# Eight key pages of the last sample in the first four attention steps, two each, and the last pair's values later

## The chip, the cores and the metric

The kernel runs on one core of one Trainium2 chip. The core has a matmul engine (TensorE, PE in the profile, its weight loads PEld), a vector engine (VectorE, DVE), a scalar engine (ScalarE, ACT), GpSimd (POOL), SyncE (SP), which here only issues loads and stores, and 16 DMA engines. Each engine takes its instructions in the order of its own queue. The metric is the device time of one execution in microseconds; lower is better. The kernel before takes 1068.47 us, the median of three runs (1067.93 to 1070.03).

## What is computed

One layer of a decoder trunk, for a prompt of 512 positions and for 8 samples of one new position each, with shared weights. The reference, cut:

```python
h = rms_norm(x, norm1_g) * (1.0 + sc1) + sh1
z = h @ w_in
xr, gr, q, k, v, fl, ga, gb = jnp.split(z, cuts, axis=-1)
xc, conv_new = causal_dwconv(xr, conv_buf, conv_w, conv_b)
hr, h_last = rg_lru(xc, h0, pos0, rg_wr, rg_br, rg_wi, rg_bi, rg_lambda)
ya = (hr.astype(x.dtype) * jax.nn.gelu(gr)) @ w_proj_a
logf = jax.nn.log_sigmoid((fl + b_f).astype(jnp.float32))
yb = attend(q, k, v, logf).reshape(B, T, ATTN_W) @ w_proj_b
mixed = (jax.nn.sigmoid(ga) * ya + jax.nn.sigmoid(gb) * yb) @ w_o
x = x + g1 * mixed
gu, up = jnp.split(h2 @ w_ffn_in, 2, axis=-1)
x = x + g2 * ((jax.nn.silu(gu) * up) @ w_ffn_out)
```

`attend` is attention with a decay from the sums of `logf`: for the prompt over its own 512 keys, for a sample over its own key and 1024 past ones. The past keys and values lie in a paged cache, 8 pages of 128 rows for each sample; a page of keys or values is 128 x 1024 floats, 512 KB:

```python
k_all = jnp.concatenate([cache_k[page_table].reshape(DB, P, N_HEADS, HEAD_DIM).astype(k.dtype), k], axis=1)
s = jnp.einsum("bqhd,bkhd->bhqk", q, k_all, preferred_element_type=jnp.float32) * scale
s = s + Fk[:, :, P:, None] - Fk[:, :, None, :]
p = jax.nn.softmax(s, axis=-1)
return jnp.einsum("bhqk,bkhd->bqhd", p.astype(v_all.dtype), v_all)
```

## The kernel before

**Products.** All large products take the 512 prompt positions and the samples together, 520 columns in two halves of 260. Operands are split in a high and a low part of 32 bits, so a product of 8 blocks of 128 rows is 2 x 8 x 3 = 48 matmuls (L245). They run in one fixed order and are numbered by `begin`: 0 and 1 are the last of `q`, then `xr` (input of the recurrence), the gate products `ga` and `gb` of the merge, and `gr`, mixed, up to 31; 32 is the first `k`; 33 to 39 and 41 are the projection `pa` of the recurrence's branch, with the first `v` between. Then come eight attention steps, then the merge (`pb`), `w_o` and the FFN.

**Weights.** A chunk of weight columns is loaded by SP into `wraw` (two buffers). ACT makes its high part `whi` (L210), DVE subtracts to give `wlo` (L211), three buffers each. `begin` runs this ahead of the product that needs it, by an estimate of time in `reach`.

**Key pages.** For the samples' past keys, a page is loaded, multiplied on DVE with the sample's query, which was broadcast to 128 partitions (`qb`, L639 and L648), and reduced by heads into `S`: two instructions of DVE a page, L667 and L668 (L663 and L664 where an entry is two half pages: the 16 entries of samples 0 and 1, each with two loads of 256 KB; samples 2 to 7 have 48 whole pages). `tick`, called by `begin` for products 0 to 41 and three or four times in an attention step, does in this order: `key_sums` for the entries loaded long enough ago, the next stage of a softmax chain, then values, then the loads of new value and key pages. `KEYS[n]` says how many key entries product n loads. Before, all 64 are loaded by product 40. `issue_after(state["last"])` ties the sums behind the last `wlo` in DVE's order.

**Softmax and values.** Samples go in pairs r = 0 to 3. When a pair's 16 pages are summed, the chain `past_softmax` runs a stage at every second tick: decays added to `S` and a maximum (`mk`, L704 to L706), a transposing matmul `lgt` (L709), `st` and `dg` on DVE (L711, L713), a matmul `lgm` (L718), a subtraction (L719), exponentials, and the weights `pw`. Then the value pages are loaded and multiplied on PE (`pv`, L751), and DVE folds them into `dr` (L757, L759). `VALUES_AT` says at which of the four places of an attention step a value is taken.

**Page pool.** Key pages, value pages, `qb` of samples 2 to 7, and the blocks `araw` of the table product `ada` (L296, L308) share one pool of seven buffers of 128 x 1024. Each takes the buffer of the seventh before it. Loads of pages are issued by POOL up to product `LAST_POOL`, then by SP.

**Recurrence.** DVE makes the convolution `xc` (L894), ACT and DVE its high and low parts `xch` and `xcl` (L278, L279), PE the recurrence's gates (`gate`, L915); later DVE scans the recurrence and splits the result in `gh` and `gl`, the input of `pa`.

**An attention step i** splits the next head pair's query (`q_split`: `qqA`, `qqB` on ACT, `qlA`, `qlB` on DVE, L1079), broadcasts decay rows, and runs the next `k` product with the step's `v` tokens in its middle, then the next `v` product with scores in its middle, and the sum with the values. `k_product`'s evacuation puts the low half of k into `ksA` and `ksB` by DVE (L1059); DVE also splits the transposed probabilities (`pl`, L1164).

The order on each engine is set by a scheduler at build time, from the order of the code, the ties of `issue_after`, and its own estimates; so an edit of `KEYS` can also move instructions that it doesn't name.

Of the kernel before, what the change touches and what calls it, by code (L numbers as in the profile page):

```python
# [64 lines left out]
def kernel(ctx, tc, xT, par, gates, b_f, cst, cse, own, cache_k, cache_v, cache_lf, pt,  # L65
# [103 lines left out]
    def flush():  # L169
        while stores:  # L170
# [1 line left out]

    later = {}

    KEYS = dict(zip(range(42), (2, 2, 2, 0, 3, 3, 3, 2, 1, 1, 1, 1, 2, 2, 2, 1, 0, 1, 0, 1, 2, 2, 2, 2, 1, 1, 1, 1, 2, 2, 1, 2,
                                1, 2, 1, 2, 1, 2, 1, 2, 1, 0)))
    VALUES = (19, 21, 23, 25, 27, 29, 31, 35, 37, 39)
    LAST_POOL = 40

    def load_chunks(upto):  # L180
        while state["dma"] < len(chunks) and state["dma"] <= upto:
            c = state["dma"]
            raw = wp.tile([128, KT, 256], F32, name="wraw", tag="wraw", bufs=2)
            o = 0
            for src, r0, nk, c0, n in chunks[c]:
                sp.dma_start(raw[:, :nk, o:o + n],
                             src[r0:r0 + nk * 128, c0:c0 + n].rearrange("(k p) c -> p k c", p=128))
                o += n
            raws[c] = raw
            state["dma"] += 1  # L190

    def split_upto(n):
        while state["split"] < len(units) and state["split"] <= n:
            m = state["split"]
            c, o, nk = units[m]
            load_chunks(c)
            raw = raws[c]
            state["split"] += 1
            his, los = [], []
            step = 4 if m in in_heap else KT  # L200
            for k0 in range(0, nk, step):
                k1 = min(nk, k0 + step)
                if m in in_heap:
                    hi = slot("whs", 512, F32R).rearrange("p (k c) -> p k c", c=128)
                    lo = slot("wls", 512, F32R).rearrange("p (k c) -> p k c", c=128)
                else:
                    hi = wp.tile([128, KT, 128], F32R, name="whi", tag="whi", bufs=3)
                    lo = wp.tile([128, KT, 128], F32R, name="wlo", tag="wlo", bufs=3)
                src = raw[:, k0:k1, o:o + 128]
                state["act"] = act.copy(hi[:, :k1 - k0], src)  # L210
                state["last"] = dve.tensor_tensor(lo[:, :k1 - k0], src, hi[:, :k1 - k0].bitcast(F32), ALU.subtract)  # L211
# [441 lines left out]
    def key_sums():  # L653
        for p in pend:
            p[0] += 1
        while pend and pend[0][0] >= state["age"]:
            _, s, j, pg, q, half = pend.pop(0)
            r = s // 2
            c = 256 * (r % 2) + 32 * j + H * (s % 2)
            with tc.issue_after(state["last"].ins):  # L660
                if half is not None:
                    b, c = 8 * (r % 2) + j, H * (s % 2) + 8 * half
                    dve.tensor_tensor(pg, pg, q.unsqueeze(1).to_broadcast([128, 2, 512]), ALU.mult)  # L663
                    dve.tensor_reduce(S[r // 2].rearrange("p (b c) -> p b c", c=32)[:, b:b + 2, c:c + 8],  # L664
                                      pg.rearrange("p j (h d) -> p j h d", d=DH), AX.X, ALU.add)
                else:
                    dve.tensor_tensor(pg, pg, q, ALU.mult)  # L667
                    dve.tensor_reduce(S[r // 2][:, c:c + H], pg.rearrange("p (h d) -> p h d", d=DH), AX.X, ALU.add)  # L668
            summed[r] += 1
            if summed[r] == 2 * NPAGE:  # L670
                chains.append([9, past_softmax(r)])
# [401 lines left out]
    def q_split(i):  # L1073
        qq = slot("qqA", NP, F32R), slot("qqB", NP, F32R)
        ql = slot("qlA", NP, F32R), slot("qlB", NP, F32R)
        for a in range(2):
            t = kvs[i]["qr"][a]
            act.activation(qq[a], t, AF.Copy, scale=-(DH ** -0.5))
            dve.scalar_tensor_tensor(ql[a], t, -(DH ** -0.5), qq[a].bitcast(F32), ALU.mult, ALU.subtract)  # L1079
# [507 lines left out]
```

## Time and profile before

| what | value |
|---|---|
| median of three runs | 1068.47 us |
| lowest and highest | 1067.93 and 1070.03 us |
| profiled execution, its own time | 1067.71 us |
| profiled execution, its span | 1066.1 us |
| mean granted clock of TensorE | 0.987 |
| ACT busy | 494.2 us (46%) |
| POOL busy | 202.2 us (19%) |
| bytes moved | 206.95 MB, mean 194 GB/s |

The profile shows one execution. The 1.6 us between its span and its own time lie before the first and after the last instruction of the span. A row of the timeline gives start, duration, engine, line, operation, what is written and read, the shape, and in brackets how long the engine was idle before and what ended that. A row of the waits gives engine and line, what was waited for, the sum in us, how often, and the longest. In the page's slices each digit is the busy share, in tenths, of one of 40 equal parts of the span (26.65 us each).

### The profile page before, as it was taken

Reading aid. Unit: us, or ns where it says so; the run is one execution under the profiler, and the core shown is the slowest. Engines: PE = TensorE matmul, PEld = TensorE weight load, DVE = VectorE, ACT = ScalarE, POOL = GpSimd, SP = SyncE. Lnnn points to the kernel's source line nnn. Section 1 sums busy time; section 2 is a strip of 40 time slices with the busy share of each in tenths; the row PEclk is TensorE's granted clock in tenths of the full one; section 3 lists DMA queues with packets and bytes.
Section 4 is the critical chain, followed back from the end, with each engine's and each line's share of the span. In section 5 each row is a group of like instructions: output and inputs, shape, how many; then the busy total and the mean of one; then the engine's idle time right before and its main releaser. Section 6 shows DMA issues by size and latency. Waiting matters only on the chain.

```text
span 1066.1 us, 21006 instructions
## 1 busy us (share of the span) xinstructions
PE 1021.3 (96%) x8210; PEld 948.1 (89%) x8210; DVE 664.0 (62%) x1166; ACT 494.2 (46%) x976; POOL 202.2 (19%) x348
## 2 busy tenths in 40 slices
PE   4999899999999999999999999999999999999994
PEld 2888779999998987888898989999999999999993
DVE  5447999988999986656765447733343333443363
ACT  4423565757782367767783235523212232123251
POOL 0224511112134234544400014100000000000022
PEclk9999899999999999999999999999999999999998
DMA  9898887778788998987746852232333332332212
GB/s 327 281 320 286 279 297 208 260 240 297 255 283 280 351 314 263 259 252 250 248 172 216 313 166 70 73 88 79 109 90 80 97 102 80 95 104 80 72 55 74
DMA packets 165285, 206.95 MB, mean 194 GB/s; under 512 B 9778, under 2 KB 126018, under 8 KB 165122
## 3 DMA queue, kind: packets, MB, share of 16 engines
q1 hardware_dynamic: 147746, 149.90, 45.6%
q0 software_dynamic: 13760, 49.29, 13.6%
q10 hardware_dynamic: 3680, 6.42, 1.6%
q8 instruction: 64, 1.05, 0.4%
q14 instruction: 35, 0.29, 0.1%
HBM read 192.49 MB, written 13.09 MB: 193 GB/s over the span
## 4 chain that ended last, share of the span: by engine, by line
PE 76%; DVE 9%; issue 4%; DMA 4%; ACT 4%; POOL 2%; POOLq 1%; SPq 0%; ACTq 0%; DVEq 0%
PE fiu L245 11%; PE fig L245 11%; PE fo L245 9%; PE pb L245 4%; PE k L245 4%; PE v L245 4%; PE pa L245 3%; PE gr L245 3%; PE gb L245 3%; PE ga L245 3%; PE xr L245 3%; PE wo L245 3%; PE pv L751 3%; DMA wraw<-in_w_in_dram 2%; PE qp L467 2%
## 5 line engine op out<-in xcount | busy, mean ns | idle before, releaser
L211 DVE TENSOR_TENSOR wlo<-wraw,whi 128x1024 fp32r<-128x1024 f32 (+1 forms) x131 | 160.7, 1227 | 159.3 <-ACT whi L210 153.2
L210 ACT CAST whi<-wraw 128x1024 fp32r<-128x1024 f32 (+1 forms) x131 | 136.7, 1043 | 242.7 <-PE fo L245 74.6
L337 POOL TENSOR_TENSOR ss<-ss,sq 128x260 f32<-128x260 f32 x18 | 13.6, 756 | 419.5 <-ACT sq L336 419.0
L245 PE MATMUL fiu<-h2h,wlo 128*128 128x260 f32 x320 | 90.5, 283 | 0.0
L245 PE MATMUL fig<-h2h,wlo 128*128 128x260 f32 x320 | 90.5, 283 | 0.0
L245 PE MATMUL fig<-h2l,whi 128*128 128x260 f32 x320 | 90.2, 282 | 0.0
L245 PE MATMUL fiu<-h2l,whi 128*128 128x260 f32 x320 | 90.2, 282 | 0.0
L245 PE MATMUL fig<-h2h,whi 128*128 128x260 f32 x320 | 90.2, 282 | 0.0
L245 PE MATMUL fiu<-h2h,whi 128*128 128x260 f32 x320 | 90.2, 282 | 0.0
L245 PE MATMUL fo<-ach,whi 128*128 128x260 f32 x292 | 82.8, 284 | 0.0
L245 PE MATMUL fo<-ach,wlo 128*128 128x260 f32 x292 | 82.5, 282 | 0.0
L245 PE MATMUL fo<-acl,whi 128*128 128x260 f32 x292 | 82.3, 282 | 0.0
L622 POOL DMA_DIRECT2D pg<-in_cache_k_dram x79 | 42.1, 533 | 115.8 <-DVE S L668 61.1
L245 PEld LDWEIGHTS fiu<-h2h,whi 128*128 128x128 f32 x320 | 60.2, 188 | 0.0
L245 PEld LDWEIGHTS fig<-h2h,whi 128*128 128x128 f32 x320 | 60.2, 188 | 0.0
L245 PEld LDWEIGHTS fig<-h2l,whi 128*128 128x128 f32 x320 | 60.2, 188 | 0.0
L245 PEld LDWEIGHTS fiu<-h2l,whi 128*128 128x128 f32 x320 | 60.2, 188 | 0.0
L245 PEld LDWEIGHTS fig<-h2h,wlo 128*128 128x128 f32 x320 | 60.1, 188 | 0.0
L245 PEld LDWEIGHTS fiu<-h2h,wlo 128*128 128x128 f32 x320 | 60.1, 188 | 0.0
L667 DVE TENSOR_TENSOR pg<-pg,qb 128x1024 f32<-128x1024 f32 x48 | 57.4, 1213 | 1.1 <-DMA pg<-in_cache_k_dram 1.0
L668 DVE TENSOR_REDUCE S<-pg 128x16 f32<-128x1024 f32 x48 | 57.2, 1207 | 0.0
L245 PEld LDWEIGHTS fo<-ach,wlo 128*128 128x128 f32 x292 | 55.1, 189 | 0.0
(388 smaller groups left out, 3445.6 us busy)
## 6 DMA issues: line engine op xcount, KB each, us to landing
araw<-in_ada_w_dram SPq DMA_DIRECT2D x48, 512.0 KB, 6.3
pg<-in_cache_k_dram POOLq DMA_DIRECT2D x47, 512.0 KB, 5.6
wraw<-in_w_fi_dram SPq DMA_DIRECT2D x44, 512.0 KB, 4.0
pg<-in_cache_v_dram SPq DMA_DIRECT2D x42, 512.0 KB, 4.9
wraw<-in_w_in_dram SPq DMA_DIRECT2D x34, 512.0 KB, 8.4
wraw<-in_w_in_dram SPq DMA_DIRECT2D x11, 1024.0 KB, 7.9
pg<-in_cache_v_dram POOLq DMA_DIRECT2D x22, 512.0 KB, 5.5
pg<-in_cache_k_dram POOLq DMA_DIRECT2D x32, 256.0 KB, 5.4
```

The costliest lines, as they stand in the source:

```text
L210: state["act"] = act.copy(hi[:, :k1 - k0], src)
L211: state["last"] = dve.tensor_tensor(lo[:, :k1 - k0], src, hi[:, :k1 - k0].bitcast(F32), ALU.subtract)
L245: state["mm"] = pe.matmul(out[:, :HALF], lhsT=wt[k], rhs=at, start=k == 0 and m == 0, stop=k == nk - 1 and m == 2)
L337: eng.tensor_tensor(acc[:, t0:t1], acc[:, t0:t1], q_, ALU.add)
L467: state["mm"] = pe.matmul(b[:, :HALF], lhsT=wt, rhs=at[:, t0:t1], start=k == 0 and m == 0, stop=k == 3 and m == 2)
L622: done.append(eng.dma_start(pg, cache[bass.ds(r, 1), :, c0:c1].rearrange("a p c -> (a p) c")))
L667: dve.tensor_tensor(pg, pg, q, ALU.mult)
L668: dve.tensor_reduce(S[r // 2][:, c:c + H], pg.rearrange("p (h d) -> p h d", d=DH), AX.X, ALU.add)
L751: pe.matmul(pv[0][32 * gq:32 * gq + 32, :], lhsT=pw[r][:, c:c + 32], rhs=pgs[gq // 2][:, 512 * hf:512 * hf + 512], start=j == 0, stop=j == ...
```

## The change

The first three edits are about the key pages.

- `KEYS` loads one entry less with products 2, 4, 5, 6, 33, 37 and 39, and one more with product 40. Six pages are left for `KEYS_AT`: two in each of the attention steps 0, 1 and 2, at the place `at(i, 2)`, by SP. `LAST_POOL` is 41 in place of 40.
- From the attention steps on, `tick` sums no pages any more (the age wanted there is 1000). Instead each step sums what is pending after `q_split` and `decay_rows`: two pages in each of steps 0 to 3, all of sample 7.
- These sums are tied: `q_split` now sets `state["last"]` to its second subtraction (`qlB`), so the multiplies come behind it; `held` puts a later weight unit's `wlo` behind the reduce, and `k_product` its `ksA` and `ksB`.

The fourth moves the values of the last pair, since its softmax chain can start only in step 3: `VALUES_AT` has two values in step 4 where it had three, and two in step 7 where it had one. The last pair's eight value pages are now taken three in step 5, three in step 6 and two in step 7, and its last fold into `dr` falls in step 7.

```diff
-    KEYS = dict(zip(range(42), (2, 2, 2, 0, 3, 3, 3, 2, 1, 1, 1, 1, 2, 2, 2, 1, 0, 1, 0, 1, 2, 2, 2, 2, 1, 1, 1, 1, 2, 2, 1, 2,
-                                1, 2, 1, 2, 1, 2, 1, 2, 1, 0)))
+    KEYS = dict(zip(range(42), (2, 2, 1, 0, 2, 2, 2, 2, 1, 1, 1, 1, 2, 2, 2, 1, 0, 1, 0, 1, 2, 2, 2, 2, 1, 1, 1, 1, 2, 2, 1, 2,
+                                1, 1, 1, 2, 1, 1, 1, 1, 2, 0)))
...
-    LAST_POOL = 40
+    LAST_POOL = 41
...
+    after = {}
+
+    def held(m):
+        return tc.issue_after(after[m].ins) if m in after else nullcontext()
...
-                state["last"] = dve.tensor_tensor(lo[:, :k1 - k0], src, hi[:, :k1 - k0].bitcast(F32), ALU.subtract)
+                with held(m):
+                    state["last"] = dve.tensor_tensor(lo[:, :k1 - k0], src, hi[:, :k1 - k0].bitcast(F32), ALU.subtract)
...
-        while pend and pend[0][0] >= state["age"]:
...
+        while pend and pend[0][0] >= (state["age"] if state["n"] < 43 else 1000):
+            key_sum()
...
+                with tc.issue_after(keys.ins) if keys else nullcontext():
+                    dve.tensor_tensor(ks[a][HEADS[1 - a], t0:t0 + n], b[pr, :n], ks[a][pr, t0:t0 + n].bitcast(F32),
+                                      ALU.subtract)
...
-            dve.scalar_tensor_tensor(ql[a], t, -(DH ** -0.5), qq[a].bitcast(F32), ALU.mult, ALU.subtract)
+            state["last"] = dve.scalar_tensor_tensor(ql[a], t, -(DH ** -0.5), qq[a].bitcast(F32), ALU.mult, ALU.subtract)
...
-    VALUES_AT = [(1, 1, 0, 1)] * 6 + [(1, 1, 0, 1), (1, 0, 0, 0)]
+    VALUES_AT = [(1, 1, 0, 1)] * 4 + [(1, 1, 0, 0)] + [(1, 1, 0, 1)] * 2 + [(1, 1, 0, 0)]
+    KEYS_AT = [(0, 0, 2, 0)] * 3 + [(0, 0, 0, 0)] * 5
...
-        tick(0, VALUES_AT[i][part])
+        tick(KEYS_AT[i][part], VALUES_AT[i][part])
...
-        (gate_b if last else k_product)(6 if last else i + 1, mid_a)
+        keys = None
+        while pend:
+            keys = key_sum()
+            after[state["split"] + 2] = keys
+        if last:
+            gate_b(6, mid_a)
+        else:
+            k_product(i + 1, mid_a, keys)
```

The body of `key_sums` moved into `key_sum`, which returns the reduce of a whole page. Three places show how the queues of DVE and PE change. A row has the line, the operation, what is written from what, and the shape; line numbers differ between the two programs, since the change adds lines.

First, DVE's queue at the first convolution and the first gates. Before (`pg` is a key entry, `xcl` what PE's gates wait for):

```order
L663 TENSOR_TENSOR pg<-pg,qb 128x1024
L537 TENSOR_SCALAR lzc<-lzc 128x8
L663 TENSOR_TENSOR pg<-pg,qb 128x1024
L538 TENSOR_TENSOR ll<-lzc,lza 128x8
L894 SCALAR_TENSOR_TENSOR xc<-xr,prm,xc 128x509
...
L894 SCALAR_TENSOR_TENSOR xc<-xr,prm,xc 128x511
L664 TENSOR_REDUCE S<-pg 128x2x8 x2
L211 TENSOR_TENSOR wlo<-wraw,whi 128x1024
L279 TENSOR_TENSOR xcl<-xc,xch 128x520
```

After the change:

```order
L673 TENSOR_TENSOR pg<-pg,qb 128x1024
L544 TENSOR_SCALAR lzc<-lzc 128x8
L537 TENSOR_SCALAR fzc<-fe 128x65
L674 TENSOR_REDUCE S<-pg 128x2x8
L545 TENSOR_TENSOR ll<-lzc,lza 128x8
L905 SCALAR_TENSOR_TENSOR xc<-xr,prm,xc 128x509
...
L905 SCALAR_TENSOR_TENSOR xc<-xr,prm,xc 128x511
L218 TENSOR_TENSOR wlo<-wraw,whi 128x1024
L286 TENSOR_TENSOR xcl<-xc,xch 128x520
```

One multiply is gone from ahead of `xc`; the reduce that is left stands ahead of `xc` and not between `xc` and `wlo`; a small row of the log-forget chain (`fzc`) moved up.

Second, DVE's queue around `dg` of pair r=2, which PE's `lgm` waits for. The `tA` rows are the sums of the `pa` products, two a product. Before, up to the sums of the second product:

```order
L667 TENSOR_TENSOR pg<-pg,qb 128x1024 x2
L668 TENSOR_REDUCE S<-pg 128x16 x2
L711 TENSOR_REDUCE st<-lgt_4595 32x1
L211 TENSOR_TENSOR wlo<-wraw,whi 128x1024
L977 TENSOR_TENSOR tA<-pa_0_4628,tA 128x260
L977 TENSOR_TENSOR tA<-pa_1_4654,tA 128x260
L667 TENSOR_TENSOR pg<-pg,qb 128x1024
L713 TENSOR_SCALAR dg<-cs,st 32x256
L668 TENSOR_REDUCE S<-pg 128x16
L211 TENSOR_TENSOR wlo<-wraw,whi 128x1024
L977 TENSOR_TENSOR tA<-pa_0_4700,tA 128x260
L977 TENSOR_TENSOR tA<-pa_1_4726,tA 128x260
```

After, from the sums of the third product to those of the fourth:

```order
L988 TENSOR_TENSOR tA<-pa_0_4741,tA 128x260
L988 TENSOR_TENSOR tA<-pa_1_4767,tA 128x260
L677 TENSOR_TENSOR pg<-pg,qb 128x1024
L722 TENSOR_REDUCE st<-lgt_4795 32x1
L678 TENSOR_REDUCE S<-pg 128x16
L724 TENSOR_SCALAR dg<-cs,st 32x256
L218 TENSOR_TENSOR wlo<-wraw,whi 128x1024
L988 TENSOR_TENSOR tA<-pa_0_4821,tA 128x260
L988 TENSOR_TENSOR tA<-pa_1_4847,tA 128x260
```

The chain has moved two products back: `dg` stood between the sums of the first and the second `pa` product, and now between those of the third and the fourth. In PE's queue `lgm` stood behind the second `pa` product, and now stands behind the fifth.

Third, DVE's queue in attention step 1, from the query's split to the low half of k. Before:

```order
L1079 SCALAR_TENSOR_TENSOR qlA<-qA,qqA 128x512
L1146 RECIPROCAL mu<-mu 128x4
L1079 SCALAR_TENSOR_TENSOR qlB<-qB,qqB 128x512
L719 TENSOR_TENSOR S<-S,lgm_5921 128x256
L211 TENSOR_TENSOR wlo<-wraw,whi 128x1024
L1059 TENSOR_TENSOR ksA<-k_0_5880,ksA 64x260
L1059 TENSOR_TENSOR ksB<-k_0_5880,ksB 64x260
L1102 TENSOR_TENSOR v_5915<-vt_5910,v_5915 128x2x128
L1059 TENSOR_TENSOR ksA<-k_1_5953,ksA 64x252
```

After:

```order
L1091 SCALAR_TENSOR_TENSOR qlA<-qA,qqA 128x512
L1158 RECIPROCAL mu<-mu 128x4
L1091 SCALAR_TENSOR_TENSOR qlB<-qB,qqB 128x512
L677 TENSOR_TENSOR pg<-pg,qb 128x1024 x2
L678 TENSOR_REDUCE S<-pg 128x16 x2
L218 TENSOR_TENSOR wlo<-wraw,whi 128x1024
L1071 TENSOR_TENSOR ksA<-k_0_5817,ksA 64x260
L1071 TENSOR_TENSOR ksB<-k_0_5817,ksB 64x260
L1114 TENSOR_TENSOR v_5852<-vt_5847,v_5852 128x2x128
L1071 TENSOR_TENSOR ksA<-k_1_5884,ksA 64x252
L1071 TENSOR_TENSOR ksB<-k_1_5884,ksB 64x252
```

Two multiplies and two reduces (L677, L678) now stand between `qlB` and `wlo`, and the subtraction of the last pair's `lgm` from `S` is gone from there; it stands in step 4.

On SP's queue, the store of the log-forget values, their spill `lfd` and the read-back `lf` (16 x 520) stood behind the four `araw` loads of the next two `ada` products (PE's at 152 and 167 us), and now stand between the first and the second of these loads. On POOL's queue, 14 page loads stand between the second and the third `qb` broadcast, where there were 16.

More of the change, by code (lines that the diff above doesn't have):

```diff
@@ L655, in key_sums, with key_sum @@
             p[0] += 1
-        while pend and pend[0][0] >= state["age"]:
[L657 to L671, printed above, removed]
+        while pend and pend[0][0] >= (state["age"] if state["n"] < 43 else 1000):
+            key_sum()
+    def key_sum():
+        _, s, j, pg, q, half = pend.pop(0)
+        r = s // 2
+        c = 256 * (r % 2) + 32 * j + H * (s % 2)
+        with tc.issue_after(state["last"].ins):
+            if half is not None:
+                b, c = 8 * (r % 2) + j, H * (s % 2) + 8 * half
+                dve.tensor_tensor(pg, pg, q.unsqueeze(1).to_broadcast([128, 2, 512]), ALU.mult)
+                dve.tensor_reduce(S[r // 2].rearrange("p (b c) -> p b c", c=32)[:, b:b + 2, c:c + 8],
+                                  pg.rearrange("p j (h d) -> p j h d", d=DH), AX.X, ALU.add)
+            else:
+                dve.tensor_tensor(pg, pg, q, ALU.mult)
+                last = dve.tensor_reduce(S[r // 2][:, c:c + H], pg.rearrange("p (h d) -> p h d", d=DH), AX.X, ALU.add)
+        summed[r] += 1
+        if summed[r] == 2 * NPAGE:
+            chains.append([9, past_softmax(r)])
+        return None if half is not None else last
     def key_pages(n):
@@ L1046, with k_product @@
     kvs = [dict() for _ in range(KT)]
-    def k_product(i, mid=None):
+    def k_product(i, mid=None, keys=None):
         t = slot("kt")
@@ L1058, in evac @@
             for a, pr in enumerate(HEADS):
-                dve.tensor_tensor(ks[a][HEADS[1 - a], t0:t0 + n], b[pr, :n], ks[a][pr, t0:t0 + n].bitcast(F32),
-                                  ALU.subtract)
+                with tc.issue_after(keys.ins) if keys else nullcontext():
+                    dve.tensor_tensor(ks[a][HEADS[1 - a], t0:t0 + n], b[pr, :n], ks[a][pr, t0:t0 + n].bitcast(F32),
+                                      ALU.subtract)
         product(f"k{i}", h, evac, mid)
@@ L1294 @@
             decay_rows(i + 1)
-        (gate_b if last else k_product)(6 if last else i + 1, mid_a)
+        keys = None
[4 more added lines that the diff above has]
+            gate_b(6, mid_a)
+        else:
+            k_product(i + 1, mid_a, keys)
         turn(i, 1 if last else 0)
```

## The prediction

> **What bounds the kernel now.** I read the page first: its busy times and its slices.
>
> ```profile
> PE 1021.3 (96%) x8210; PEld 948.1 (89%) x8210; DVE 664.0 (62%) x1166; ACT 494.2 (46%) x976; POOL 202.2 (19%) x348
> ...
> PE   4999899999999999999999999999999999999994
> ...
> DVE  5447999988999986656765447733343333443363
> ```
>
> TensorE (PE) is the bound: 1021.3 of 1066.1 us busy, with the same matmuls before and after the change. So the change can only win what PE loses by waiting or by a lower clock. VectorE (DVE) is full from slice 5 to slice 12, about 105 to 320 us, and half empty afterwards. The waits of PE between 100 and 480 us say what can be won:
>
> ```profile
> PE gate L915 <- DVE xcl L279: 2.8, 1, 2.8
> PE ada L308 <- DMA araw<-in_ada_w_dram: 2.3, 2, 1.8
> PE lgm L718 <- DVE dg L713: 1.8, 1, 1.8
> PE gate L915 <- ACT xch L278: 1.3, 1, 1.3
> PE pa L245 <- DVE gl L279: 1.1, 2, 0.6
> PE ga L245 <- DVE wlo L211: 0.9, 1, 0.9
> ```
>
> They lie at three places of the stretch in which DVE is full: the first recurrence gates, the table product `ada` behind `xr3`, and the products `pa` with the softmax chain of pair r=2. I take them in that order.
>
> **First gates (105 to 128 us).** PE's own timeline:
>
> ```profile
> 114.10 0.28 PE L245 MATMUL ga<-hl,whi 128*128 128x260 f32 x1
> 115.69 0.50 PE L915 MATMUL gate<-xch,gws 128*128 128x260 f32 x2 [1.31 <-ACT xch L278]
> 119.03 0.58 PE L915 MATMUL gate<-xcl,gws 128*128 128x260 f32 x1 [2.83 <-DVE xcl L279]
> ...
> 121.36 0.42 PE L245 MATMUL ga<-hh,whi 128*128 128x260 f32 x1
> ...
> 128.17 0.28 PE L245 MATMUL ga<-hl,whi 128*128 128x260 f32 x1
> ...
> 129.73 0.28 PE L245 MATMUL gb<-hh,whi 128*128 128x260 f32 x1
> ...
> 135.38 0.28 PE L245 MATMUL gb<-hl,whi 128*128 128x260 f32 x1
> ```
>
> From the last matmul of `ga` to the first of the next one pass 7.26 us (114.10 to 121.36) with twelve gate matmuls between; the second time the same twelve take 1.56 (128.17 to 129.73). So 5.70 are lost. The product after it takes 6.81 (121.36 to 128.17), the next 5.65 (129.73 to 135.38): 1.16 more, at matmuls of 0.42 instead of 0.28, a lower clock. The cause stands on DVE:
>
> ```profile
> 108.61 1.21 DVE L663 TENSOR_TENSOR pg<-pg,qb 128x1024 f32<-128x1024 f32 x1
> ...
> 111.31 1.31 DVE L663 TENSOR_TENSOR pg<-pg,qb 128x1024 f32<-128x1024 f32 x1 [1.16 <-DMA pg<-in_cache_k_dram]
> ...
> 112.62 0.73 DVE L894 SCALAR_TENSOR_TENSOR xc<-xr,prm,xc 128x509 f32<-128x509 f32 x1
> ...
> 114.24 0.73 DVE L894 SCALAR_TENSOR_TENSOR xc<-xr,prm,xc 128x511 f32<-128x511 f32 x1
> 114.91 2.33 DVE L664 TENSOR_REDUCE S<-pg 128x16 f32<-128x1024 f32 x2
> 117.16 1.20 DVE L211 TENSOR_TENSOR wlo<-wraw,whi 128x1024 fp32r<-128x1024 f32 x1
> 118.29 0.68 DVE L279 TENSOR_TENSOR xcl<-xc,xch 128x520 fp32r<-128x520 f32 x1
> ```
>
> Two key entries stand around the convolution `xc`; the second waits 1.16 us for its page, with `xc` queued behind it, and both reductions stand ahead of `xcl`. Product 2 now loads one entry, and DVE's new order is multiply, reduce, `xc`, `wlo`, `xcl`. Walked with these durations: the multiply is through at 109.75, three small rows take 0.3, the reduce 1.13, so `xc` starts at about 111.25 and its third tap at 112.87 (1.62 later, as from 112.62 to 114.24 in before); `xch` reaches PE 1.45 after that, as before, at 114.3; `wlo` runs from 113.5, `xcl` from 114.7, and PE has it 0.74 later, as before, at 115.4. PE then waits 0.1 and 0.85 in place of 5.70. **Term 1: 5.70 + 1.16 - 0.95 = 5.9 us**, if the clock stays up.
>
> **The table product (150 to 155 us).**
>
> ```profile
> 150.34 0.28 PE L245 MATMUL xr<-hl,whi 128*128 128x260 f32 x1
> ...
> 154.99 0.39 PE L245 MATMUL gr<-hh,whi 128*128 128x260 f32 x1
> ...
> 166.60 0.28 PE L245 MATMUL xr<-hl,whi 128*128 128x260 f32 x1
> ...
> 167.81 0.39 PE L245 MATMUL gr<-hh,whi 128*128 128x260 f32 x1
> ...
> 142.83 1.22 DVE L664 TENSOR_REDUCE S<-pg 128x16 f32<-128x1024 f32 x1
> ...
> 146.23 2.34 DVE L664 TENSOR_REDUCE S<-pg 128x16 f32<-128x1024 f32 x2
> ...
> 147.47 6.49 DMA araw<-in_ada_w_dram
> ```
>
> Eight `ada` matmuls take 4.65 us at one place and 1.21 at the other: 3.4 lost. The last row is from the chain of waits: the load starts at 147.47, when the first of the reduces from 146.23 is through, since `araw` takes buffers of the page pool, seven in all. Four entries fewer are loaded up to there (products 2, 4, 5, 6). So the two `araw` loads take the slots of entries that come five earlier in DVE's list, which my walk frees at about 129.7 and 134.9. One thing moves against it: on SyncE's (SP) queue the log-forget store, its spill and the read-back `lf` now stand between the two loads, and `lf` waits for the spill. Walked on DVE, `fa` is written at 130.9; with the spill the second load goes at about 136.8, and with the 6.49 of the chain it lands at 143.3. PE, 5.9 earlier, needs it at 144.8. **Term 2: 3.4 us**, with 1.5 us of cover; if the read-back is 3 us later, half of the term goes.
>
> **Pair r=2 (316 to 336 us).**
>
> ```profile
> 328.00:332.00 4.00, 2.17 (x18) 1.31 (x11) 4.00 (x6) 0.65 (x1) 4.00 (x8) 1.00 1.15 262
> 332.00:336.00 4.00, 4.00 (x23) 4.00 (x23) 4.00 (x6) 0.00 (x0) 0.52 (x1) 0.57 0.83 247
> 336.00:340.00 4.00, 4.00 (x36) 4.00 (x35) 4.00 (x7) 1.44 (x2) 1.05 (x2) 1.00 1.04 410
> ```
>
> The windows give span, busy time and count of PE, PEld, DVE, ACT and POOL, granted clock, DMA share and GB/s. After the 1.83 wait for `dg` the clock falls to 0.57, and 23 matmuls pass instead of 36: 13 x 0.12 = 1.6 us. (0.12 is the pitch of matmuls between 129.73 and 135.38: 5.65 over 47.) In the new order `lgm` stands behind the fifth `pa` product, where it was behind the second, while `dg` on DVE is behind the third: the wait goes, and the clock loss with it, 3.4. Of the 1.1 for `gl`, I count 0.3: the sums of r=2 (`S`, `mk`) leave the queue ahead of `gl`, but PE's order there is tighter now. The matmul `lgt` is next in line, with about 1 us of margin. **Term 3: 3.7 us.**
>
> **What is paid in the attention steps.** The six pages are not saved. In steps 0 to 3 two multiplies and two reduces stand between `qlB` and the weight's `wlo`:
>
> ```profile
> 357.33 2.35 DVE L667 TENSOR_TENSOR pg<-pg,qb 128x1024 f32<-128x1024 f32 x2
> 359.60 2.34 DVE L668 TENSOR_REDUCE S<-pg 128x16 f32<-128x1024 f32 x2
> 361.86 1.21 DVE L211 TENSOR_TENSOR wlo<-wraw,whi 128x1024 fp32r<-128x1024 f32 x1
> ...
> 410.97 1.41 DVE L211 TENSOR_TENSOR wlo<-wraw,whi 128x1024 fp32r<-128x1024 f32 x1 [4.73 <-DMA pg<-in_cache_v_dram]
> ...
> 429.03 0.69 DVE L1079 SCALAR_TENSOR_TENSOR qlB<-qB,qqB 128x512 fp32r<-128x512 f32 x1
> 434.68 1.23 DVE L211 TENSOR_TENSOR wlo<-wraw,whi 128x1024 fp32r<-128x1024 f32 x1 [4.96 <-ACT whi L210]
> ```
>
> A pair takes 361.86 - 357.33 = 4.53 us. The idle time at that place is 4.96 in step 2 and 4.73 in step 1, where the subtraction of `lgm` ahead of it goes as well: they fit, by 0.2 to 1 us. Behind the reduces, in DVE's order, are `wlo`, the low halves of k (`ksA`, `ksB`), v, the scores' `pl` and the decays. `wlo` itself is for a product a step later; but `pl` is waited for by PE at once. Step 3 also holds the pair r=2's fold (`dr`). The cost is bounded by nothing, where all fits, and 4 x 4.53 = 18.1, where nothing does; I take the near end, since the idle rows are longer than the pair: 0.15 a step, **0.6 us**. Below nothing it cannot go, since no work of these steps is taken out. The other move, the last pair's values into steps 5 to 7, keeps the counts of loads and folds, and the steps that get them have DVE at 5 to 7 tenths in the slices above; a late fold there could cost between nothing and the 0.6 once more, and I take nothing. The six key loads on SP add 1 MB to each of three steps.
>
> **Sum.** 5.9 + 3.4 + 3.7 - 0.6 = 12.4 us. Against the profiled execution, 1067.71, that is 1055.3; the median of the three runs is 0.76 higher, 1068.47, so I predict **1056.0**.
>
> **The rivals.**
> - **The waits come back a little later** (chance 0.20). PE arrives up to 9 us earlier at places where DVE is still full, and the term of the table or that of pair r=2 is met by the next late load. For it: the DMA share is 0.83 to 1.15 in the windows above. Against it: DVE sheds four entries (9.7 us at 2.42 an entry) ahead of the places where PE gains 9.3, so their distance stays. If terms 2 and 3 fall, 12.4 - 7.1 = 5.3 is left: 1063.2.
> - **The clock falls all the same** (0.10). Its dips in before followed waits of 2.83 and 1.83 us, but 1.79 and 0.54 at the table product were followed by full clock:
>
> ```profile
> 152.00:156.00 4.00, 3.04 (x16) 1.30 (x17) 4.00 (x6) 3.59 (x6) 0.53 (x1) 1.00 0.93 331
> ```
>
>   So the length of a wait does not settle it. If both dips stay, 1.16 + 1.6 = 2.8 are not won: 1058.8. [...]
> - **The keys don't quite fit** (0.15). If a pair ends 1 us behind its idle time in each of four steps, `pl` is late by that and PE waits at the scores: 4 instead of 0.6, 1059.5.
> - **Slower** (0.08). The pairs wait for their own pages or their broadcast query at the head of DVE's queue, with `ksA`, `ksB` and `pl` behind them, and are exposed wholly: 18.1 - 13.0 = 5.1 lost, 1073.6. It decides from 13.0 / 4 = 3.25 us exposed per step. For it: loads beside the weights took up to 6.49 us above. Against it: the pages are asked for a step ahead, and a step is 23.7 us (from the `wlo` at 410.97 to that at 434.68).
> - **No change** (0.05). The order on DVE shows fewer keys ahead of the first gates, so it does what it says; but if `xcl` comes late for another reason (its weight's `whi`, held by PE's progress), and the key steps cost as in the third rival, about 1 us remains: 1067.5.
>
> **How the numbers follow.** The forecast has 0.42. The range takes it, with the first three rivals: 0.87 in all, from 1053.5, where the steps cost nothing (0.6) and the rests of terms 1 and 3 (0.95 and 0.8) go as well, to 1063.5, just past the first rival. A measurement of this kernel tells about 0.2% (2.1 us) from no change. Faster: 0.42 + 0.20 + 0.10 + 0.15 = 0.87; same 0.05; slower 0.08.
>
> **What would show it.** Term 1: `xcl` behind one reduce, PE's wait for it below 1.2 us, and about 84 to 88 matmuls from 112 to 123 us with the clock at 1.00. Term 2: no `ada` row among PE's waits, the second `araw` issued at 135 to 138. Term 3: no wait at `lgm`, and no window below 1.00 around it. Steps 0 to 3: DVE's idle time ahead of `wlo` nearly gone but still there, and no new PE waits for `pl` or `ksA` of over 0.3 us. I am wrong if PE's waits before 340 us still sum to over 5 us, or if those between 380 and 480 exceed 4.

## Result, and the profile after

The changed kernel takes **1063.67 us**, the median of seven runs (1061.09 to 1064.31); the kernel before took 1068.47 in seven runs beside it (1067.23 to 1071.49). The ratio is **0.9946**, 95% interval [0.9931, 0.9961]: 4.8 us faster, where 12.4 were forecast, and 0.2 us above the range. The profiled execution of the changed kernel took 1063.58, its span 1061.9, 4.2 less than before.

From the page of the changed kernel (span in 40 slices of 26.55 us):

```profile
PE 1020.2 (96%) x8210; PEld 946.4 (89%) x8210; DVE 666.2 (63%) x1166; ACT 493.3 (46%) x976; POOL 206.4 (19%) x343
...
DVE  5447999988989878867654558633343333443363
```

DVE is a little emptier in slices 12, 14 and 15 and fuller in 16 to 19 (about 398 to 504 us): key sums have moved into the attention steps. PE's waits between 100 and 480 us, in the same view as before:

```profile
PE gate L926 <- ACT gate L927: 1.8, 1, 1.8
PE v L252 <- DVE pl L1176: 1.3, 2, 1.0
PE ga L252 <- DVE wlo L218: 1.0, 1, 1.0
PE sc L1148 <- DVE pl L1176: 0.7, 4, 0.2
PE pa L252 <- DVE gl L286: 0.7, 1, 0.7
PE ptt L1171 <- ACT ph L1175: 0.6, 1, 0.6
PE gate L926 <- DVE xcl L286: 0.6, 1, 0.6
...
PE gate L926 <- ACT xch L285: 0.2, 1, 0.2
```

`ada` and `lgm` are gone, `xcl` fell from 2.8 to 0.6. New are a wait for ACT at the gates, and waits for `pl` and `ph` in the attention steps.

PE runs the same matmuls in the same numbering of products, so the start of one matmul can be compared in the two traces. The table, from PE's timelines, has the matmul that starts a stretch; "lead" is after minus before, and negative is sooner.

| matmul | before | after | lead | what lies in between |
|---|---|---|---|---|
| `xr`, first one | 95.52 | 96.41 | +0.89 | |
| `ga` ahead of the first gates | 108.46 | 109.70 | +1.24 | |
| `ga` behind them, clock up again | 123.95 | 119.65 | -4.30 | 5.5 won (term 1) |
| `gr` behind the table product | 154.99 | 147.23 | -7.76 | 3.5 won (term 2) |
| `gr` | 273.91 | 266.14 | -7.77 | |
| `gr` behind the gates at 282 us | 302.49 | 298.03 | -4.46 | **3.3 lost** |
| `pa` ahead of `lgm` | 319.05 | 313.81 | -5.24 | 0.8 won (`gl`) |
| `pa` behind `lgm` and the clock's dip | 334.57 | 325.63 | -8.94 | 3.7 won (term 3) |
| `pa` | 351.03 | 342.75 | -8.28 | |
| `v`, step 0 | 393.31 | 387.32 | -5.99 | **2.3 lost** |
| `k`, behind steps 1 and 2 as well | 406.72 | 400.09 | -6.63 | nothing lost up to 459 |
| `v`, step 3 | 463.67 | 459.41 | -4.25 | **2.4 lost** |
| last matmul of the FFN | 1048.79 | 1045.07 | -3.72 | 1.4 lost, 2.1 won, 1.2 lost, small steps |

So the three terms were won, and three places that had cost little before took more than half of it again.

**The places that were won, and the gates at 282 us.** PE's timeline at the first gates, at the table product, and at the second gates:

```profile
115.33 0.28 PE L252 MATMUL ga<-hl,whi 128*128 128x260 f32 x1
115.81 0.51 PE L926 MATMUL gate<-xch,gws 128*128 128x260 f32 x2 [0.20 <-ACT xch L285]
116.90 0.39 PE L926 MATMUL gate<-xcl,gws 128*128 128x260 f32 x1 [0.58 <-DVE xcl L286]
...
118.21 0.28 PE L252 MATMUL ga<-hh,whi 128*128 128x260 f32 x1
...
146.24 1.07 PE L315 MATMUL ada<-araw,silc 128*32 128x512 f32 x8
147.23 0.39 PE L252 MATMUL gr<-hh,whi 128*128 128x260 f32 x1
...
279.67 1.06 PE L762 MATMUL pv<-pg,pw 128*32 128x512 f32 x8
282.57 0.51 PE L926 MATMUL gate<-xch,gws 128*128 128x260 f32 x2 [1.84 <-ACT gate L927]
```

From `ga` to `ga` pass 2.88 us where 7.26 passed, and the eight `ada` run without a wait. The windows around pair r=2's old dip and at the new one (busy time and count of PE, PEld, DVE, ACT, POOL, clock, DMA share, GB/s):

```profile
280.00:284.00 4.00, 2.16 (x17) 1.43 (x10) 4.00 (x5) 3.97 (x8) 1.60 (x4) 0.91 0.39 131
284.00:288.00 4.00, 4.00 (x25) 4.00 (x25) 4.00 (x6) 1.64 (x5) 1.03 (x2) 0.67 0.95 321
...
328.00:332.00 4.00, 3.86 (x33) 3.69 (x32) 3.27 (x6) 1.58 (x2) 1.73 (x4) 1.00 1.03 410
332.00:336.00 4.00, 4.00 (x36) 3.23 (x34) 4.00 (x7) 0.68 (x1) 0.53 (x1) 1.00 1.02 412
```

332 to 336 has 36 matmuls where it had 23, and the clock is 1.00 from 318 to 345 us, where `lgm` and the `pa` around it now run. The dip is now at 284, with 25.

**Loss at 282 us.** These are the second recurrence gates, of products 28 and 29. ACT's timeline:

```profile
279.15 0.63 ACT L285 CAST gh<-ge 128x520 fp32r<-128x520 f32 x1 [1.06 <-DVE ge L957]
279.68 1.04 ACT L216 CAST whi<-wraw 128x1024 fp32r<-128x1024 f32 x1
280.74 1.28 ACT L927 ACT_TABLE_LOAD   x1
282.04 1.58 ACT L927 ACTIVATE gate<-gate,prm 128x260 f32<-128x260 f32 x4
```

PE is through with `pv` at 280.73, wants a free `gate` bank, and gets it at 282.57. Ahead of the activation that frees it stand, in ACT's queue, a weight's cast (1.04) for a later product, and the load of the sigmoid's table (1.28). In before the cast stood at 280.27, ahead of `xch`, and PE came late enough not to wait (its `gate` matmuls run from 288.46 on). Of the 3.3 us lost, 1.84 are this wait; the rest, 1.4, is the dip of the clock behind it.

**Losses in steps 0 and 3.** DVE's timeline in step 0 (three rows), step 1 (four) and step 3 (four):

```profile
384.24 1.29 DVE L1176 TENSOR_TENSOR pl<-ptt,ph 128x512 fp32r<-128x512 f32 x2
385.45 1.21 DVE L218 TENSOR_TENSOR wlo<-wraw,whi 128x1024 fp32r<-128x1024 f32 x1
386.58 1.88 DVE L1176 TENSOR_TENSOR pl<-ptt,ph 128x512 fp32r<-128x512 f32 x3
...
400.50 2.35 DVE L677 TENSOR_TENSOR pg<-pg,qb 128x1024 f32<-128x1024 f32 x2
402.77 2.33 DVE L678 TENSOR_REDUCE S<-pg 128x16 f32<-128x1024 f32 x2
405.03 1.43 DVE L218 TENSOR_TENSOR wlo<-wraw,whi 128x1024 fp32r<-128x1024 f32 x1
406.49 0.42 DVE L1071 TENSOR_TENSOR ksA<-k,ksA 64x260 fp32r<-64x260 f32 x1
...
451.32 1.44 DVE L218 TENSOR_TENSOR wlo<-wraw,whi 128x1024 fp32r<-128x1024 f32 x1 [0.33 <-ACT whi L216]
452.68 0.96 DVE L715 TENSOR_TENSOR S<-S,suf 128x128 f32<-128x128 f32 x2
453.68 0.62 DVE L717 TENSOR_REDUCE mk<-S 128x32 f32<-128x256 f32 x1
454.31 0.42 DVE L1071 TENSOR_TENSOR ksA<-k,ksA 64x260 fp32r<-64x260 f32 x1
```

And in before, the `wlo` at the same places of step 0 and step 3:

```profile
386.84 1.35 DVE L211 TENSOR_TENSOR wlo<-wraw,whi 128x1024 fp32r<-128x1024 f32 x1 [2.05 <-ACT whi L210]
457.76 1.23 DVE L211 TENSOR_TENSOR wlo<-wraw,whi 128x1024 fp32r<-128x1024 f32 x1 [4.91 <-ACT whi L210]
```

In step 0 a `wlo`, meant for a later product, stands in the middle of the five `pl`; the wait of 1.0 for `pl` at `v`, in the list above, is at that place (387.32). In step 1 the pair, `wlo` and `ksA` follow each other without a gap, and PE loses nothing. In step 3 the first stage of pair r=3's softmax chain (`S`, `mk`, 1.6 us) comes in between `wlo` and `ksA`, because r=3 is now summed in this step (in before that stage ran from 383.44 to 384.80, in step 0); everything behind it, down to `pl`, is that much later. The idle time of 4.91 in before has room for the pair (4.6), not for the pair and 1.6.

### The profile page after: what moved, and what is told of

Read it like the earlier page. It is cut to its first block, busy times and chain, and to the rows that moved or that the text cites. A ratio compares the mean times of both kernels' runs of the same rounds, so it can differ in the third digit from the quotient of the medians.

```text
span 1061.9 us, 21017 instructions
## 1 busy us (share of the span) xinstructions
PE 1020.2 (96%) x8210; PEld 946.4 (89%) x8210; DVE 666.2 (63%) x1166; ACT 493.3 (46%) x976; POOL 206.4 (19%) x343
## 3 DMA queue, kind: packets, MB, share of 16 engines
q0 software_dynamic: 13040, 46.67, 13.5%
## 4 chain that ended last, share of the span: by engine, by line
PE 74%; DVE 11%; ACT 5%; DMA 5%; issue 3%; POOL 1%; SPq 0%; POOLq 0%; DVEq 0%; ACTq 0%
PE fiu L252 11%; PE fig L252 11%; PE fo L252 10%; PE pb L252 4%; PE gb L252 4%; PE xr L252 3%; PE ga L252 3%; PE v L252 3%; PE k L252 3%; PE pa L252 3%; PE wo L252 3%; DMA wraw<-in_w_in_dram 2%; PE gr L252 2%; DVE wlo L218 2%; PE qp L474 2%
## 5 line engine op out<-in xcount | busy, mean ns | idle before, releaser
L629 POOL DMA_DIRECT2D pg<-in_cache_k_dram x74 | 39.4, 533 | 141.4 <-DVE S L678 68.6
L677 DVE TENSOR_TENSOR pg<-pg,qb 128x1024 f32<-128x1024 f32 x48 | 58.0, 1226 | 2.5 <-DMA pg<-in_cache_k_dram 2.5
L678 DVE TENSOR_REDUCE S<-pg 128x16 f32<-128x1024 f32 x48 | 57.0, 1206 | 0.1
```

The source lines that it names most:

```text
L629: done.append(eng.dma_start(pg, cache[bass.ds(r, 1), :, c0:c1].rearrange("a p c -> (a p) c")))
L678: last = dve.tensor_reduce(S[r // 2][:, c:c + H], pg.rearrange("p (h d) -> p h d", d=DH), AX.X, ALU.add)
```

## Experiments

Each ratio is to the kernel before, timed beside the run (medians 1068.5 to 1070.5 us), so across runs the ratios compare better than the medians.

**b2: the early part of the change alone.** On the kernel before, products 2, 4, 5 and 6 load one entry less, and 16, 18, 19 and 20 one more; no page goes to the attention steps.

```diff
-    KEYS = (2, 2, 2, 0, 3, 3, 3, 2, 1, 1, 1, 1, 2, 2, 2, 1, 0, 1, 0, 1, 2, ...
+    KEYS = (2, 2, 1, 0, 2, 2, 2, 2, 1, 1, 1, 1, 2, 2, 2, 1, 1, 1, 1, 2, 3, ...
```

> The kernel before, with one key entry less at products 2, 4, 5 and 6, and one more at 16, 19, 20 and 18's neighbour places (products 16, 18, 19, 20 take 1, 1, 2, 3); nothing of the attention steps is changed. Theory (terms 1 and 2 hang on the early entries alone): the gates and the table product win 5.2 + 3.4 us, 1059.5 to 1061. Rival (DVE is full up to 320 us and only shifts the waits): new waits of PE between 170 and 320 us give most of it back, 1064 to 1069.

Measured: 1065.3, ratio 0.9959 [0.9943, 0.9974].

```profile
PE gate L915 <- ACT gate L916: 3.0, 1, 3.0
PE lgm L718 <- DVE dg L713: 1.7, 1, 1.7
PE pa L245 <- DVE gl L279: 1.2, 2, 0.8
```

Terms 1 and 2 are won without the attention steps (PE leads by 10.8 us behind the table product), and `lgm`'s wait stays. The gates at 282 us take 4.3 of it back: that loss is no effect of the moved pages, but of PE's earlier arrival. So the time is the rival's, though the new wait of over 1 us is one alone, at these gates. Nothing is lost between 387 and 480 us, so the losses in steps 0 and 3 do come with the pages, with their sums or with the order that they bring. In time this part alone can't be told from the whole change (0.9959 against 0.9946, the intervals overlap).

**x1 and x5: the exponential at 275 us.** ACT loads tables at 273.55, for the exponential of the weights `pw` of pair r=1, and at 275.27, back for the gelu `ge`, 1.28 us each. x1 starts that chain later, x5 makes one stage of it sooner.

```diff
-            chains.append([9, past_softmax(r)])
+            chains.append([9 if r != 1 else 0, past_softmax(r)])              # x1
+            chains.append([9, past_softmax(r), [1] if r == 1 else []])        # x5
...
-                    c[0] = 0
+                    c[0] = c[2].pop() if c[2] else 0                          # x5
```

> The changed kernel, with the softmax chain of pair r=1 started one tick later, so that its exponential no longer stands between the two halves' gelu of the last gr product ahead of the gates. Theory (placement): the two table loads there held ACT back, the second set of gate matmuls waited 1.84 us for it and the clock fell after it: both go, 3.2 us, from 1063.7 to about 1060.5, no wait at gate for ACT, and no window below 1.00 near 282 us. Rival (the high parts and the weight's cast keep ACT late anyhow): at most one table load is won, 1062.5 to 1063.7, and the wait at gate stays above 0.8.

> The changed kernel, with the second stage of pair r=1's chain one tick sooner, so that its exponential falls in the xr product ahead of the last gr, before both halves' gelu. Theory (placement on ACT): the two table loads between the gelus become one ahead of them, and the second set of gate matmuls near 282 us no longer waits 1.84 us; with the clock 2 to 3.2 us, 1060.5 to 1061.7. Rival (the gates wait there in any order, since the weight's cast stands ahead of the gelu and its load lands only at 270 to 275 us): a wait of over 0.8 us remains at those gates, 1062.7 to 1064.

Measured: x1 1063.3, 0.9944 [0.9928, 0.9960]; x5 1060.17, 0.9901 [0.9877, 0.9925]. In x1 the gates wait 1.8 for the chain's `S` on DVE in place of ACT, and step 0 loses about 2 us more. In x5 the exponential is out of the way, and yet the wait is 2.1:

```profile
278.61 1.05 ACT L216 CAST whi<-wraw 128x1024 fp32r<-128x1024 f32 x1 [1.98 <-PE ga L252]
279.56 0.62 ACT L285 CAST gh<-ge 128x520 fp32r<-128x520 f32 x1
280.20 1.28 ACT L927 ACT_TABLE_LOAD   x1
281.49 1.58 ACT L927 ACTIVATE gate<-gate,prm 128x260 f32<-128x260 f32 x4
```

So my first theory, the exponential's table, falls. What both orders have is the cast ahead of the table load. x5's time came out as the theory had it, but not for its reason: its trace still loses 3.7 us at the gates and gains 1.2 us at step 0; why was not tried.

**x6: the cast behind the gates.** One tie on ACT; `gt` is the last gate activation.

```diff
-                state["act"] = act.copy(hi[:, :k1 - k0], src)
+                with tc.issue_after(state["gt"].ins) if state["n"] == 29 else nullcontext():
+                    state["act"] = act.copy(hi[:, :k1 - k0], src)
...
```

> The changed kernel, with the weight cast whi of product 28's begin tied on ACT behind the four gate activations near 282 us; the exponential of pair r=1 stays where it is. Theory (the cast, 1.04 us ahead of the gates' table load, is what keeps the gates waiting, since x5 moved the exponential and the wait stayed): the wait of 1.84 falls to 0.8 or less, and 1 to 2.5 us are won, 1061.2 to 1062.7. Rival (ACT waits for DVE's ge, and the gates are late with any order on ACT): the wait stays above 1.4, 1063 to 1064.

Measured: **1057.68**, 0.9883 [0.9859, 0.9907]. ACT's timeline in x6:

```profile
277.80 0.63 ACT L286 CAST gh<-ge 128x520 fp32r<-128x520 f32 x1 [1.68 <-DVE ge L958]
278.44 1.28 ACT L928 ACT_TABLE_LOAD   x1
279.74 1.58 ACT L928 ACTIVATE gate<-gate,prm 128x260 f32<-128x260 f32 x4
281.19 1.07 ACT L217 CAST whi<-wraw 128x1024 fp32r<-128x1024 f32 x1
```

The wait falls to 0.9 and the clock stays at 1.00. `lgt` of pair r=2 then waits 1.2 for a `whi`; the changed kernel has no such wait in its first profile and 0.7 in its second. But in x6 the order of step 0 also changed: the second `wlo` stands ahead of the last `v` and all `pl`, and ACT takes `qqB` ahead of two `p` rows of 1.2 us, so that the pair starts sooner. The wait for `pl` is gone there, so the gain has two parts, and the time is 3.5 us below the theory's.

**x6w, x63, x63g: the parts apart.** All have x6's tie. x6w holds two `wlo` of step 0 between the second and third `pl` (one more than the changed kernel has there); x63 holds step 0's `wlo` behind all `pl`; x63g does that in step 3 too.

```diff
+            if i == 0:                               # x63g: if i in (0, 3)
+                state["lead"] = 8                 # x6w: this block stands ahead of turn(i, 1)
+                after[state["split"]] = state["pl"]
+                split_upto(reach(state["n"] - 1, len(units) - 1, 8))
...
```

> Product 28's weight cast on ACT is tied behind the gate activations as in x6_cast_behind_gates, and step 0's two wlo are held between the second and third pl, as they stand in the changed kernel, so that only the cast differs. Theory 'the cast ahead of the gates costs 3.2 us': the wait for the gate at 282 us stays below 1.0 us with the clock at 1.00 in 280 to 292 us, step 0 loses the 2 us that it loses in the changed kernel, and the time is 1060.5 (1063.7 - 3.2). Rival 'the gain of x6 came from where wlo fell in step 0': 1063.7 as the changed kernel, with the gate's wait gone all the same and the lead lost again by step 0.

> The cast tied as in x6_cast_behind_gates and step 0's wlo held behind all pl. Theory 'two separate losses of 3.2 and 2.0 us': no wait for pl above 0.3 us at step 0's v, and 1058.3 (1063.7 - 3.2 - 2.2). Rival 'PE meets the next late row': step 0's gain is given back by 480 us and the time is that of x6w_cast_only.

> As x63_cast_and_wlo, and step 3's wlo held behind pl too, so that the mask row of pair r=3 and ksA come 1.2 us sooner there. Theory 'step 3's 2.4 us are the DVE rows ahead of ksA': about 1.2 us of the 2.4 at step 3 are won against x63_cast_and_wlo, if wlo's own product does not wait. Rival 'step 3 waits for something else, or wlo is then late': no gain, a new wait for wlo.

Measured: x6w 1058.82, 0.9894 [0.9875, 0.9913]; x63 1057.86, 0.9895 [0.9878, 0.9912]; **x63g 1057.6**, 0.9890 [0.9872, 0.9909]. The gates wait 0.9 us in all three, at full clock. At step 0's `v`, x6w waits 2.4 and x63 not at all; from the first `v` to there x63 gains 2.4 us against the changed kernel. DVE in step 0 of x63 (two rows) and in step 3 of x63g:

```profile
380.44 1.89 DVE L1177 TENSOR_TENSOR pl<-ptt,ph 128x512 fp32r<-128x512 f32 x3 [1.44 <-ACT ph L1176]
382.24 1.22 DVE L219 TENSOR_TENSOR wlo<-wraw,whi 128x1024 fp32r<-128x1024 f32 x1
...
444.39 1.08 DVE L716 TENSOR_TENSOR S<-S,suf 128x128 f32<-128x128 f32 x2
445.50 0.63 DVE L718 TENSOR_REDUCE mk<-S 128x32 f32<-128x256 f32 x1
446.15 0.42 DVE L1072 TENSOR_TENSOR ksA<-k,ksA 64x260 fp32r<-64x260 f32 x1
```

In x63 DVE idles ahead of the last `pl`, which shows that the pair alone doesn't make step 0 late. In x63g `S` follows the pair at once, `ksA` comes sooner, and the trace gains 1.5 us at that `v` against x63's; no later product waits for the `wlo`. So step 3 does hang on the rows ahead of `ksA`. In the timed medians the three can't be told apart (their intervals overlap nearly wholly), and x6w's profiled execution, 1064.48, was the slowest of its five, so its trace doesn't show its median. Yet x6w, whose step 0 loses more than the changed kernel's, has a lower ratio than both timings of the changed kernel (0.9946, and 0.9927 in s1 below, whose interval overlaps), so the tie on the cast very likely wins time by itself.

**x3: only step 0's `wlo` behind `pl`,** without x6's tie (x63's edit).

> The changed kernel, with the second weight's wlo of attention step 0 tied behind the five pl, where it stood between the second and the third. Theory (placement): 1.1 us of wlo go from ahead of the last pl, the wait of v for pl falls from 1.0 to about 0.3, 1.2 to 1.7 us: 1062.0 to 1062.5. Rival (the key pair itself makes step 0 late): the wait stays at 0.8 or more, 1063.2 to 1064.

Measured: 1060.66, 0.9912 [0.9889, 0.9934]. Step 0 won 2.4, as in x63. Its profiled execution, 1067.33, was again the slowest: ACT stood 8.62 us for a weight load, up to 275.19.

**x4: no late sums.**

> The changed kernel with the multiplies and reduces of the eight pages in the attention steps left out: each is replaced by a short copy of 16 columns, the loads stay, so the last sample's scores are not computed. It shows what the key pairs cost in all: theory (their cost is the two placements of steps 0 and 3, for which DVE's idle time was the cover) 2.0 + 2.4 = 4 us, 1059.3 to 1060.3. Rival (steps 1 and 2 pay too, or the loads do): over 5.5 us, below 1058; or under 2 us, above 1061.7, if the loads and not the sums are what is paid.

Measured: 1058.66, 0.9891 [0.9866, 0.9915], between the theory and the rival. But the kernel leaves out six pages and not eight: the copies begin at 399.69 us, in step 1, and step 0 still sums its pair.

```profile
373.95 2.35 DVE L680 TENSOR_TENSOR pg<-pg,qb 128x1024 f32<-128x1024 f32 x2
```

Without the pair of step 3 its loss is nearly gone (1.8 of 2.2 us won, from 455 us of before on). Step 0's wait of 1.0 for `pl` stays, with pair and `wlo` as in the changed kernel, so x4 says nothing on step 0; x3 and x63 do: with the same pair and the `wlo` behind the `pl`, the wait is gone. The profiled execution, 1060.92, was the slowest of six.

**x2 and x2c: the chain of r=3 behind `pl`.** Step 3's `S` and `mk` are tied behind the last `pl`; x2c also moves the read-back `mb` on SP's queue behind the decay rows of step 7.

```diff
-            chains.append([9, past_softmax(r)])
+            chains.append([{3: -1}.get(r, 9), past_softmax(r)])
...
+        with tc.issue_after(state["pl"].ins) if r == 3 else nullcontext():
```

> The changed kernel, with the first stage of pair r=3's chain (two additions to S, a maximum) two ticks later and tied behind the last pl of attention step 3. Theory (placement): these 1.6 us ahead of ksA, not the key pairs, cost step 3 its 2.4 us: 1061.3 to 1062, and PE keeps its lead through step 3 within 0.5 us. Rival (the two key pages do not fit in a step): step 3 still loses over 1.5 us, 1063 to 1064.

> As x2_chain3_behind_pl, with the read-back mb of the last pair's sums on SP's queue moved behind the decay rows of step 7. Theory: the 2.6 us that x2 won in step 3 stay, and its loss of 5 us at gb, where SP stood 8 us at mb with the decay rows behind it, goes: 1060.8 to 1061.5. Rival (the loss at gb comes from the later values of the last pair): the wait at gb stays, 1065 to 1066.

Measured: x2 1065.97, 0.9963 [0.9948, 0.9978]; x2c 1062.35, 0.9922 [0.9897, 0.9948]. Step 3 won 2.1 in x2, but a later product (`gb`, near 540 us) lost 5.0: DVE held the probabilities of step 6 until the store of a key had finished.

```profile
530.99 0.29 DVE L1156 CUSTOM_DVE_ANT_0 p<-f,sc 128x128 f32<-128x128 f32 x1 [2.55 <-DMA out_kT_dram<-kt]
```

In x2c's profile that loss was 6.7 with `mb` moved, so it comes without `mb` too. But that execution, 1067.25, was the slowest of six, and the median is near the theory's time: whether the others had the loss, and what made the store late, is open.

**Sums of edits.** x53 joins x5 and x3; x536 adds x6's tie; x123 joins x1, x2 and x3; z joins x5, x2c and x3.

> x5 and x3 together. Theory (both gains are real and lie apart): 1060.2 - 1.2 to 2.4 = 1058.0 to 1059.0, PE's wait of v for pl in step 0 below 0.4. Rival (x5's median is a draw of the chip): 1060 to 1061.5.

> x5, x3 and x6 together: no exponential between the gelus, the cast behind the gates, wlo of step 0 behind pl. Theory: no wait of over 0.8 us of the gates near 282 us and no low clock there: 1055.5 to 1057.5, near the forecast of 1056.0. Rival (DVE's ge keeps ACT late): as x53, 1058 to 1060.

> The three edits of the other runs together. Theory (placement): the gains add, 3.2 + 2 + 1.5 = 6.7 us: about 1057.0, and PE's lead over the kernel before stays above 9 us from 350 us to the end of the attention steps. Rival (keys or loads do not fit): at most the gain of the first edit remains, 1060 to 1063.

> x5, x3 and x2c together: pair r=1's exponential sooner, wlo of step 0 behind pl, the sums of pair r=3 behind pl of step 3, mb behind the decay rows. Theory (three placements cost what the forecast lacked): 1063.7 - 2.5 - 2.4 - 2.6 = 1056.2, within 1.5. Rival (DVE or the loads have no time for the key pairs): no better than x3 alone, 1060 to 1062.

Measured: x53 1062.76, 0.9930 [0.9906, 0.9954]; x536 1060.87, 0.9907 [0.9880, 0.9934]; x123 1067.69, 0.9975 [0.9960, 0.9990]; z 1061.88, 0.9913 [0.9887, 0.9938]. None adds up. x123 and z have x2's loss at `gb`, in profiled executions that were the slowest of their runs; x53 keeps the gates' wait of 2.1, and by its interval it is not clearly apart from x5 or x3 alone. x536 has x6's short wait (0.8) at full clock, and yet isn't faster than x6; why is open.

**s1 and s2: the changed kernel and x6 again,** on one chip.

> The changed kernel itself, beside the next run on the same chip. Theory 'the start up to 110 us is scatter of executions, the losses at 282 us, step 0 and step 3 belong to the order': 1063.7 within 1.5, a wait for the gate of about 1.8 us with a clock below 0.7 behind it, and waits at step 0 and step 3 as in its first profile, while ga's start near 109.7 us may lie up to 2 us sooner. Rival 'its first timing was a slow chip or placement': 1060 or less, and the waits at those places gone.

> The same kernel as x6_cast_behind_gates, on the chip of s1_changed_kernel. Theory 'the cast and the order of wlo that it brings are worth 5 to 6 us': 1057.7 to 1058.5. Rival 'its trace's 1.3 us net of the wait that comes back at lgt, plus 2 us of step 0, are all': 1060.4, and the rest was scatter between chips.

Measured: s1 1062.17, 0.9927 [0.9900, 0.9954]; s2 1058.88, 0.9885 [0.9863, 0.9908]. So on one chip the tie is worth 3.3 us by the medians. From the gates to the end of step 0, s2's trace gains 3.9 on s1's: 0.9 at the gates, 2.4 in step 0 (a wait for `pl` and a dip of the clock), the rest at `pa`. The windows of s1 show why the gates gave less here:

```profile
280.00:284.00 4.00, 3.13 (x25) 3.14 (x26) 4.00 (x5) 3.93 (x11) 1.59 (x3) 1.00 0.83 270
284.00:288.00 4.00, 4.00 (x36) 4.00 (x35) 4.00 (x5) 2.81 (x4) 0.53 (x1) 1.00 0.92 331
384.00:388.00 4.00, 3.71 (x19) 3.71 (x20) 2.70 (x12) 2.09 (x9) 0.08 (x1) 0.62 1.04 346
```

The same kernel had the same wait of 1.83 us at the gates, but the clock stayed up behind it, and fell in step 0 instead.

## Why the prediction was wrong

- **Terms 1 and 2 were right, to 0.4 us:** 5.5 won against 5.9, 3.5 against 3.4. `xcl`'s wait came out at 0.58 where 0.85 was walked; the second `araw` load went at 138.7 where 136.8 was walked, still in time.
- **Term 3 was right too:** 3.7 at `lgm` and the clock against 3.4, 0.8 at `gl` against 0.3. Together the three won 13.5 in the trace, against 13.0.
- **The step that failed is "What is paid in the attention steps", 0.6 us.** It measured 4.7: 2.3 in step 0, 2.4 in step 3. The reason given, that the idle rows are longer than the pair, holds for steps 1 and 2, the ones whose rows were read, and they cost nothing. For steps 0 and 3 no idle row was read. Step 3's is as long (4.91), but the step has a work of its own that the prediction missed: it named r=2's fold there, but not the first stage of r=3's chain, which the change itself brings into that step. Without that stage (x2), without the `wlo` ahead of it (x63g) or without the pair (x4), most of the loss is gone. Step 0's row is 2.05, beside work that the change takes away; there a `wlo` lands among the `pl`, and x3 and x63 show that with it behind them the same pair costs nothing.
- **What is late next was looked for on DVE only.** The first rival said that PE would come up to 9 us earlier where others are still full, and set against it that DVE sheds its work sooner as well. It did. ACT didn't: behind its cast and table load the gates at 282 us cost 3.3. b2 shows that the place comes with PE's earlier arrival; x6 shows that the cast makes 0.9 of the wait, and that 0.9 stay without it. No term had this place. The first rival's time, 1063.2, is near the result, but its mechanism, that terms 2 or 3 fall, did not occur.
- **The clock.** That waits of 1.79 and 1.83 us were followed by 1.00 and 0.57 was said, and priced as a rival. Here its dips went at the two old places (1.00 from 112 to 124 us and from 328 to 336), and one came at a new one (0.67 from 284 to 288).
- **Its own signs.** Neither sign of being wrong was met: the listed waits sum to 4.3 us from 100 to 340 us (5 was the mark) and to 2.8 from 380 to 480 (4 was the mark). The list holds no dip of the clock, and its sums are smaller than the 8 us that the starts of matmuls lose at the three places. The sign for steps 0 to 3 was met: a new wait of 1.0 for `pl`, where 0.3 was the mark.
- **The rest.** 13.5 - 3.3 - 4.7 = 5.5. PE's late start up to the first gates, 1.2 in the profiled execution, and 0.6 of small steps later leave 3.7 at the last matmul; the spans differ by 4.2. The start is mostly scatter: s1, the same kernel, begins `xr` 1.6 us sooner, at 94.79, and is 1.7 sooner at the gates (280.87 against 282.57).
- **Open:** how much the tie is worth exactly. By their ratios x6, x63 and x63g are 5.4 to 6.7 us (of 1068) faster than the changed kernel's 0.9946, s2 is 4.5 faster than s1 by ratio and 3.3 by median, with step 0's part in it; the intervals, 2 to 3 us to each side, hold all of these.

## What to carry to other kernels

Once a bound engine has been moved several us ahead, read the queue of every engine at its later meeting places, not only the one that was relieved: here the next late row was a weight's cast that nobody needed yet, ahead of a table load, and one tie behind the gates, with the order that it brought into step 0, took the kernel to 1057.7, and to 1058.9 in a second timing. For a step repeated in four places, read the rows of all four, and list what the change itself makes fall due there: in step 3 the idle time alone looked long enough. Judge small reorderings one by one and again together, since their gains did not add.

## What the runs showed of the hardware

**Waits of the same length were followed by different clocks.** Of the ten profiled executions whose gates at 282 us waited 1.8 to 2.1 us (the changed kernel twice, x1, x2, x2c, x4, x5, x53, x123, z), six show a window below 0.85 at 280 to 288 us (their lowest are 0.64 to 0.77) and four show 1.00 throughout; the changed kernel is in both groups. At step 0 its wait of 1.0 us was followed by 1.00 in one execution and 0.62 in the other. All six executions with x6's tie (x6, x6w, x63, x63g, x536, s2), with waits of 0.8 to 0.9 there, show 1.00. The dip at the gates in the changed kernel and the one at step 0 in s1 cost 1.4 to 1.5 us each: by that much PE's lead falls from the first gate matmuls behind the wait (282.57) to the `gr` at 298.03 in the changed kernel, and from the `v` of step 0 to the end of its dip in s1. What decides whether and when a dip comes isn't shown: six of the ten single waits of 1.8 to 2.1 us were followed by one, and so was step 0 of s1, where no single wait was longer than 1.0.
